# Output projection with w_out held whole in two parts, token tiles finished one by one, and a ring of 23 weight slots

## The chip, the cores and the metric

The kernel runs on one core of one Trainium2 chip. The metric is the device time of one execution in microseconds (us). The kernel before takes 1562.64 us, the median of 3 runs (1561.81 to 1563.06).

## What is computed

One encoder block on 512 tokens of width 1024, in float32: two kinds of attention, a merge, an output projection, and a mixture of 16 experts in which every expert picks its 64 tokens.

```python
h = _rms_norm(x, attn_norm_w)
z = einsum('btd,dc->btc', h, w_in)      # latent q, kv, diff q, k, v, two gates
o_mla  = 16 heads of latent attention
o_diff = 8 heads, softmax(q1 k1) - lam * softmax(q2 k2), times v
merged = sigmoid(g_mla + b0) * o_mla + sigmoid(g_diff + b1) * o_diff
x  = x + einsum('btc,cd->btd', merged, w_out)          # the output projection
h2 = _rms_norm(x, ffn_norm_w)
affinity  = softmax(einsum('btd,de->bte', h2, router_w))
gate, idx = top_k(swapaxes(affinity, 1, 2), 64)        # tokens of each expert
ye = (silu(xe @ w_gate) * (xe @ w_up)) @ w_down * gate # 16 experts, xe = h2[idx]
x  = x + scatter_add(idx, ye)
```

## The kernel before

The 512 tokens are four tiles of 128 (t = 0 to 3); the width of 1024 is eight blocks of 128 (k or c = 0 to 7). A float32 product of the first part is made of three: each operand is split into a high part of type float32r (an ACT copy) and the rest (a subtraction on DVE or POOL), and `proj3` (lines 195 to 202) sums high by high, high by low and low by high on TensorE (PE). A split of a weight is `w_split` (lines 122 to 131): load, ACT copy at line 129, subtraction at line 130.

The order of the program is: input projection and latent attention (to about 320 us), then eight differential heads (`diff_proj` projects a head's q, k and v, `diff_head` does its attention, `finish` adds it, gated, to the merge `mrg`), then the output projection and the router, then the experts. A scheduler interleaves neighbouring pieces on each engine, so that products of the output projection fill PE while head 7, the last, waits for other engines. Each engine and each DMA queue works through its list in order. Nearly all loads go through the queue of SP.

The output projection (lines 644 to 803) goes by halves of the columns, n = 0 and 1. For a half, four pieces of w_out (128x2x512, 512 KB each) are loaded and split (`wo_split`), the merge is split for each token tile into `mt` (lines 705 to 710), and 24 products per tile are summed over the eight blocks. The first half goes over k = 0 to 6 for all four tiles and then k = 7, the block of head 7. In the second half each tile is evacuated into `xm` (which holds x and becomes x plus the projection), transposed (`xm_part`) and routed (`route`: logits `lg`, softmax, `aff`, and its transpose). After the last tile a chain of maxima (`largest`, lines 805 to 816) finds the threshold of each expert, and the first expert's tokens are gathered by products with a one-hot matrix (`xeTp`, line 904).

The expert weights are 384 chunks of 1 MiB: for each expert eight of w_gate, eight of w_up, eight of w_down. `chunks()` (lines 678 to 696) issues them on SP, each into the next slot of a ring. ORDER (line 32) is a string with a letter per slot: m is the memory of the merge, h of its splits, e, a, x and b, c other places that come free at the end of the heads or of the projection. A chunk's load waits until the last reader of its slot is done; when PE has used a chunk (eight products `gu` at line 943 or `y` at line 976) its slot takes a new one. The first five chunks stand in SP's list ahead of two pieces of w_out (`raw1`, lines 700 to 702), which go through a slot of kind a.

Of the kernel before, what the change touches and what calls it, by code (L numbers as in the profile page):

```python
# [16 lines left out]
OP = mybir.AluOpType  # L17
# [14 lines left out]
ORDER = "eeeemmaxaaaahhhhbbbbbc"  # L32
NRE, NRA, NRB = (ORDER.count(c) for c in "eab")
# [13 lines left out]
def build(tc, A, out):  # L47
# [41 lines left out]
    with ExitStack() as es:  # L89
# [9 lines left out]
        wpool = prj.enter_context(tc.tile_pool(name="w", bufs=1, reuse_waits="tile"))  # L99
# [526 lines left out]
        V.tensor_tensor(rw, rw, vT[:, FN:FN + 8, None].to_broadcast([128, KT, NE]), OP.mult)  # L626

# [13 lines left out]
        pb.__exit__(None, None, None)  # L641
        pb3.close()

# [4 lines left out]
        wpool = att.enter_context(tc.tile_pool(name="wo", bufs=1, reuse_waits="tile"))  # L648

        def wo_view(n, i):  # L650
            return w_out[:, 2 * i:2 * i + 2, n * 512:(n + 1) * 512]

        def wo_split(n):
            return [w_split(wo_view(n, i), (128, 2, 512), eng=G if n == 0 and i == 3 else None,
                            raw=raw1[:, i - 2] if n == 1 and i > 1 else None) for i in range(4)]

        sc = wpool.tile([NE, 1024], F32, name="sc")
        wo0 = wo_split(0)
        mt_ = [ringH.tile([128, 2, KT, 128], F32R, name="mt", tag="wh", bufs=NT) for _ in range(NT)]
# [14 lines left out]

        def slot_tile(pool, tag, n, shape=(128, FF)):
            return pool().tile(list(shape), F32, name="w" + tag, tag=tag, bufs=n)

        def chunks():

            i = 0  # L680
            for e in range(NE):
# [3 lines left out]
                for src in srcs:  # L685
                    pool, tag, n = rings[order[i]]
                    i += 1
                    w = slot_tile(pool, tag, n)
# [8 lines left out]

        stream = chunks()
# [6 lines left out]
        for c0, c1 in ((0, 2), (2, 4), (4, 6), (6, 7), (7, 8)):  # L705
            for t in range(NT):
                hi, lo = mt_[t][:, 0, c0:c1], mt_[t][:, 1, c0:c1]
                m = mrgs[c0 // 4][:, c0 % 4:(c1 - 1) % 4 + 1, t * 128:(t + 1) * 128]
                S.activation(hi, m, AF.Copy)
                V.tensor_sub(lo, m, hi.bitcast(F32))  # L710
# [68 lines left out]
        for n in range(2):  # L779
            wo = wo0 if n == 0 else wo_split(1)  # L780
            if n == 0:
                wps = [ps_tile(g_, "wo") for g_ in ("pj", "pj", "s", "s")]
                for ks in (range(7), range(7, 8)):
                    for t in range(NT):
                        wo_part(wps[t], t, wo, ks)
                for t in range(NT):
                    wo_evac(wps[t], t, 0)
# [225 lines left out]
```

## Time and profile before

| | |
|---|---|
| median of the runs | 1562.64 us |
| lowest and highest of 3 | 1561.81 and 1563.06 us |
| the profiled execution | 1563.41 us, of which the span of the trace is 1561.7 us |
| busy in the span | PE 1436.0 us (92%), DVE 567.5 (36%), ACT 376.8 (24%), POOL 158.3 (10%) |
| moved by DMA | 448.55 MB |

The profiled execution lies 0.8 us above the median; 1.7 us of it lie outside the span. All positions below are microseconds from the span's start. PE is TensorE, DVE VectorE, ACT ScalarE, POOL GpSimd, and SPq the queue of loads that SP issues. The page cuts the span into 40 slices of 39 us; a digit there is a busy share in tenths.

### The profile page before, as it was taken

The page shows a single profiled execution, that of the slowest core. Times are in us where ns is not written, and L with a number is a line of the kernel's source. Part 1 is how long each engine was busy: PE and PEld are TensorE (multiplying, and loading weights), DVE is VectorE, ACT ScalarE, POOL GpSimd, SP SyncE. Part 2 cuts the span into 40 slices and gives each one's busy share as a digit, 9 for nine tenths or more (in the row PEclk, how much of TensorE's full clock was granted, in tenths as well). Part 3 has the DMA queues.
Part 4 walks back from the last instruction along what each step waited for, and adds up shares of the span by engine and source line. Part 5 has one row for each costly group of instructions (what it writes and reads, how often), then busy time and mean ns, then how long its engine had stood idle before and what let it go on. Part 6 is the DMA issues. An engine that isn't in the chain of part 4 may idle for free. (4 is left out here: it accounts for less than half of the span.)

```text
span 1561.7 us, 18429 instructions
## 1 busy us (share of the span) xinstructions
PE 1436.0 (92%) x7119; PEld 780.2 (50%) x7119; DVE 567.5 (36%) x1412; ACT 376.8 (24%) x830; POOL 158.3 (10%) x213
## 2 busy tenths in 40 slices
PE   8999999999999897899999979889879979979876
PEld 6776767788888676434333333223224224215211
DVE  7966646538888886202102002002002002002100
ACT  4545545536566653000000000000000000000000
POOL 3003203023434410000000000000000000000000
PEclk9999999999999999899999999999999999999999
DMA  4412113122212268899999999999999999999997
GB/s 157 128 52 62 58 35 109 38 89 61 75 49 58 69 229 319 333 421 424 420 421 424 420 421 425 422 423 421 420 423 424 419 424 423 422 423 420 419 418 293
DMA packets 125691, 448.55 MB, mean 287 GB/s; under 512 B 9734, under 2 KB 51778, under 8 KB 92579
## 3 DMA queue, kind: packets, MB, share of 16 engines
q1 hardware_dynamic: 124160, 444.30, 71.6%
q0 software_dynamic: 1440, 3.07, 0.7%
q8 instruction: 56, 0.92, 0.2%
q14 instruction: 33, 0.26, 0.0%
q10 hardware_dynamic: 2, 0.00, 0.0%
HBM read 441.57 MB, written 5.77 MB: 286 GB/s over the span
## 5 line engine op out<-in xcount | busy, mean ns | idle before, releaser
L955 DVE TENSOR_TENSOR hh<-hh,gu 128x512 f32<-128x512 f32 x32 | 22.0, 687 | 432.3 <-PE gu L943 432.3
L943 PE MATMUL gu<-wwa,xeT 128*64 128x512 f32 x560 | 129.8, 599 | 14.2 <-DMA wwa<-in_expert_w_up_dram 8.2
L943 PE MATMUL gu<-wwb,xeT 128*64 128x512 f32 x520 | 121.6, 599 | 15.6 <-DMA wwb<-in_expert_w_up_dram 8.1
L943 PE MATMUL gu<-wwe,xeT 128*64 128x512 f32 x496 | 117.5, 601 | 15.6 <-DMA wwe<-in_expert_w_up_dram 9.0
L943 PE MATMUL gu<-wwh,xeT 128*64 128x512 f32 x432 | 101.3, 599 | 11.3 <-DMA wwh<-in_expert_w_gate_dram 6.5
L952 ACT ACTIVATE hh<-gu 128x512 f32<-128x512 f32 x32 | 19.0, 597 | 343.3 <-PE gu L943 343.3
L943 PEld LDWEIGHTS gu<-wwa,xeT 128*64 128x64 f32 x560 | 37.4, 136 | 102.3 <-issue 66.2
L201 PE MATMUL dqkv<-hl,hTh 128*128 128x384 f32 x256 | 88.2, 345 | 0.3 <-DVE hl L510 0.3
L200 PE MATMUL dqkv<-hl,hTh 128*128 128x384 f32 x256 | 87.3, 342 | 0.0
L882 POOL DMA_DIRECT2D out_dram<-acc x4 | 2.2, 558 | 828.8 <-DVE acc L878 828.8
L202 PE MATMUL dqkv<-hl,hTl 128*128 128x384 f32 x256 | 85.6, 339 | 0.0
L943 PEld LDWEIGHTS gu<-wwb,xeT 128*64 128x64 f32 x520 | 34.6, 136 | 100.5 <-issue 59.6
L976 PE MATMUL y<-wwb,hh 128*64 128x512 f32 x320 | 74.1, 599 | 7.2 <-DMA wwb<-in_expert_w_down_dram 7.2
L943 PEld LDWEIGHTS gu<-wwe,xeT 128*64 128x64 f32 x496 | 32.5, 137 | 94.4 <-issue 52.8
L963 ACT ACTIVATE hh<-hTp 128x512 f32<-128x512 f32 x16 | 9.6, 597 | 277.7 <-PE hTp L960 277.7
L943 PEld LDWEIGHTS gu<-wwh,xeT 128*64 128x64 f32 x432 | 28.7, 136 | 80.8 <-issue 51.4
L976 PE MATMUL y<-wwa,hh 128*64 128x512 f32 x280 | 63.7, 597 | 4.2 <-DMA wwa<-in_expert_w_down_dram 4.0
L904 PE MATMUL xeTp<-ohr,xm 128*128 128x128 f32 x512 | 62.6, 282 | 1.3 <-DVE ohr L891 1.3
L904 PEld LDWEIGHTS xeTp<-ohr,xm 128*128 128x128 f32 x512 | 59.8, 196 | 7.6 <-issue 6.3
L875 PE MATMUL comb<-yo 128*128 128x512 f32 x112 | 57.4, 625 | 4.1 <-ACT yo L988 4.1
L989 DVE COPY yo<-y 64x512 f32<-64x512 f32 x14 | 9.7, 694 | 140.4 <-ACT yo L988 140.3
L976 PE MATMUL y<-wwh,hh 128*64 128x512 f32 x240 | 55.1, 598 | 3.6 <-DMA wwh<-in_expert_w_down_dram 3.6
(356 smaller groups left out, 2562.5 us busy)
## 6 DMA issues: line engine op xcount, KB each, us to landing
wwb<-in_expert_w_down_dram SPq DMA_DIRECT2D x39, 1024.0 KB, 18.0
wwa<-in_expert_w_gate_dram SPq DMA_DIRECT2D x36, 1024.0 KB, 19.8
wwb<-in_expert_w_up_dram SPq DMA_DIRECT2D x35, 1024.0 KB, 19.5
wwa<-in_expert_w_down_dram SPq DMA_DIRECT2D x35, 1024.0 KB, 20.0
wwa<-in_expert_w_up_dram SPq DMA_DIRECT2D x34, 1024.0 KB, 19.8
wwe<-in_expert_w_gate_dram SPq DMA_DIRECT2D x32, 1024.0 KB, 19.6
wwb<-in_expert_w_gate_dram SPq DMA_DIRECT2D x30, 1024.0 KB, 19.6
wwe<-in_expert_w_up_dram SPq DMA_DIRECT2D x30, 1024.0 KB, 19.6
```

The source lines that it names most:

```text
L200: PE.matmul(p, sh, mh, start=first and k == 0, stop=False)
L201: PE.matmul(p, sh, ml, start=False, stop=False)
L202: PE.matmul(p, sl, mh, start=False, stop=last and k == n - 1)
L875: PE.matmul(p, ohT[:, t * 128:(t + 1) * 128], ysp[:, n], start=True, stop=True)
L882: G.dma_start(out2[t * 128:(t + 1) * 128], acc[t // 2][:, t % 2])
L904: PE.matmul(p[:, k], xm[:, t, kk * 128:(kk + 1) * 128], ohr[:, t].rearrange("p a s -> p (a s)"), start=t == 0, stop=t == NT - 1)
L943: PE.matmul(pp[j][hf * 64:(hf + 1) * 64], cur[:, k, par_ * 64:(par_ + 1) * 64], wt[:, hf * 1024 + j * 512:hf * 1024 + (j + 1) * 512], star ...
L952: S.activation(hid[:, j * 512:(j + 1) * 512], pp[j], AF.Silu)
L955: V.tensor_tensor(hs, hs, gu[1][j], OP.mult)
L963: S.activation(dst, p, AF.Copy)
L976: PE.matmul(y[a * 64:(a + 1) * 64], hT[:, f, hf * 64:(hf + 1) * 64], wt[:, j, a * 512:(a + 1) * 512], start=kt == 0, stop=kt == 15)
L989: V.tensor_copy(ysp[own, 1], y[64:])
```

## The change

- The whole of w_out is held as hi and lo, in four pairs of blocks (`wo_`), instead of half of it at a time. Pair 0 is loaded and split between the latent attention and the differential heads, into a new place `ringW`. Pairs 1 and 2 are loaded raw during the heads, into the place that x will have, and split in the last heads; pair 3 is loaded late into places of the heads' tiles. The subtractions go by the rule `G if k or i == 0 else V`: five on POOL, three on DVE.
- x (`xm`) is loaded after those splits, during the last heads, instead of before the heads.
- The pool "w" of weight pieces is closed behind the latent attention and opened again as "w2".
- The merge is split in whole blocks of 512 tokens (`mt_split`), blocks 1, 3 and 5 on POOL.
- For tiles 0 and 1 the products of k = 0 to 5 are summed ahead, evacuated by ACT with the factor 0.5 and added into xm by POOL; for tile 2 they stay in PSUM. Then the tiles are finished one by one: both halves of the columns, evacuation, transposes, routing. Tile 3 has all its 48 products there. The last rsqrt of the routing is on DVE instead of POOL.
- ORDER has 23 slots in a new order; w stands for ringW. Ten chunks are issued ahead of the rest of the program's order, and no piece of w_out stands between them.
- The memory set aside for dynamic DMA is 4096 bytes instead of the default.

```diff
-ORDER = "eeeemmaxaaaahhhhbbbbbc"
-NRE, NRA, NRB = (ORDER.count(c) for c in "eab")
+ORDER = "mxeeaaaaambbbbbbhhhhwwc"
+NR = {c: ORDER.count(c) for c in ORDER}
...
+        prjw.close()
+        wpool = prjw.enter_context(tc.tile_pool(name="w2", bufs=1, reuse_waits="tile"))
...
-        xm = xpool.tile([128, NT, D], F32, name="xm")
-        for t in range(NT):
-            SY.dma_start(xm[:, t], x_in[t * 128:(t + 1) * 128])
...
+        def wo_pair(i, pool, tag, raw):
+
+            hi, lo = (pool.tile([128, 2, D], F32R, name="wo", tag=tag, bufs=NR[tag[1]]) for _ in range(2))
+            for k in range(2):
+                S.activation(hi[:, k], raw[k], AF.Copy)
+                (G if k or i == 0 else V).tensor_tensor(lo[:, k], raw[k], hi[:, k].bitcast(F32), OP.subtract)
+            return hi, lo
+
+        raw = xpool.tile([128, 2, D], F32, name="raw", tag="xm", bufs=1)
+        SY.dma_start(raw, w_out[:, 0:2])
+        wo_ = [wo_pair(0, ringW, "ww", [raw[:, k] for k in range(2)])]
+        raw = xpool.tile([128, NT, D], F32, name="raw", tag="xm", bufs=1)
+        SY.dma_start(raw, w_out[:, 2:6])
...
+        wo_ += [wo_pair(i, ringB, "wb", [raw[:, 2 * i - 2 + k] for k in range(2)]) for i in range(1, 3)]
+        xm = xpool.tile([128, NT, D], F32, name="xm", tag="xm", bufs=1)
+        for t in range(NT):
+            SY.dma_start(xm[:, t], x_in[t * 128:(t + 1) * 128])
...
+        def mt_split(c):
+            hi, lo = mth[c // 4][:, c % 4], mtl[c // 4][:, c % 4]
+            S.activation(hi, mrg(c), AF.Copy)
+            (G if c % 2 and c < 6 else V).tensor_tensor(lo, mrg(c), hi.bitcast(F32), OP.subtract)
...
+        for t in range(2):
+            for n in range(2):
+                p = ps_tile("pj", "wo")
+                wo_part(p, t, n, range(6))
+                part = mo2.tile([128, 512], F32, name="part", tag="ohr" if n else "oh", bufs=1)
+                S.activation(part, p, AF.Copy, scale=0.5)
+                xs = xm[:, t, n * 512:(n + 1) * 512]
+                G.tensor_tensor(xs, xs, part, OP.add)
+        wp2 = [ps_tile("pj", "wo") for n in range(2)]
+        for n in range(2):
+            wo_part(wp2[n], 2, n, range(6), last=False)
+        raw = [pb1p.tile([128, D], F32, name="raw", tag="qk2", bufs=2),
+               pbp.tile([128, D], F32, name="raw", tag="qkv", bufs=3)]
+        for k in range(2):
+            SY.dma_start(raw[k], w_out[:, 6 + k])
+        wo_.append(wo_pair(3, ringB, "wb", raw))
...
-        early = [next(stream) for _ in range(5)]
-        raw1 = slot_tile(*rings["a"], shape=(128, 2, 2, 512))
-        for i in range(2):
-            SY.dma_start(raw1[:, i], wo_view(1, 2 + i))
-        early += [next(stream) for _ in range(2)]
+        early = [next(stream) for _ in range(10)]
...
-            rr = rsqrt1(mo, st[:, 1:2], "rr", G if t == NT - 1 else V)
+            rr = rsqrt1(mo, st[:, 1:2], "rr")
...
+        for t in range(NT):
+            wps = wp2 if t == 2 else [ps_tile("s", "wo") for n in range(2)]
+            xT = xTs[:, t % 2]
+            for n in range(2):
+                wo_part(wps[n], t, n, range(8) if t == 3 else range(6, 8), first=t != 2)
+                if n:
+                    xm_part(t, 0, 4, xT, S)
+                wo_evac(wps[n], t, n, 1 + n)
+            xm_part(t, 4, 2, xT, V)
+            xm_part(t, 6, 2, xT, S)
+            route(t, xT)
...
-    nc = bacc.Bacc("TRN2", target_bir_lowering=False, num_devices=1)
+    nc = bacc.Bacc("TRN2", target_bir_lowering=False, num_devices=1, dynamic_dma_scratch_size=4096)
```

The list of SP, from the last pieces of w_out to the end of the first lap of slots (wm, wwx, wwe and so on are chunks in slots of those kinds, gB a gate that a head reads), before:

```order
L127 DMA wr<-in_w_out_dram 128x2x512 x4
L695 DMA wm_6081<-in_expert_w_gate_dram 128x2048
L695 DMA wwx<-in_expert_w_gate_dram 128x2048
L695 DMA wwe<-in_expert_w_gate_dram 128x2048 x4
L702 DMA wwa<-in_w_out_dram 128x2x512 x2
L695 DMA wm_6086<-in_expert_w_gate_dram 128x2048
L695 DMA wwa<-in_expert_w_gate_dram 128x2048
L695 DMA wwa<-in_expert_w_up_dram 128x2048 x4
L695 DMA wwh<-in_expert_w_up_dram 128x2048 x4
L695 DMA wwb<-in_expert_w_down_dram 128x2x1024 x5
L695 DMA wwc<-in_expert_w_down_dram 128x2x1024
L695 DMA wwe<-in_expert_w_down_dram 128x2x1024 x2
```

And now:

```order
L667 DMA xm<-in_x_dram 128x1024 x4
L698 DMA raw<-in_w_out_dram 128x1024
L740 DMA wm_6242<-in_expert_w_gate_dram 128x2048
L740 DMA wwx<-in_expert_w_gate_dram 128x2048
L740 DMA wwe<-in_expert_w_gate_dram 128x2048 x2
L740 DMA wwa<-in_expert_w_gate_dram 128x2048 x4
L740 DMA wwa<-in_expert_w_up_dram 128x2048
L740 DMA wm_6260<-in_expert_w_up_dram 128x2048
L740 DMA www<-in_expert_w_down_dram 128x2x1024
L740 DMA wwb<-in_expert_w_up_dram 128x2048 x6
L740 DMA wwh<-in_expert_w_down_dram 128x2x1024 x4
L740 DMA wwc<-in_expert_w_down_dram 128x2x1024
```

The chunks in slots of kinds h and b have changed places, x and one block of w_out stand ahead of the first chunk, and the chunk of slot w stands ahead of those of b.

The list of POOL from the last copy KH of head 6 to the last biases of head 7 (L529 and L533 normalise head 7's q and k, L564 and L568 are the biases by distance), before:

```order
L553 COPY KH<-KH 64x512
L564 TENSOR_SCALAR bias<-dist 128x512 x4
L534 TENSOR_SCALAR gB<-gB 128x512
L529 TENSOR_TENSOR qk_5730<-qkv,rq_y 128x256 x4
L130 TENSOR_TENSOR hl<-wr,hl 128x1024
L564 TENSOR_SCALAR bias<-dist 128x512 x2
```

And now (L634 is the subtraction of a w_out block, L674 that of a merge block, L691 the addition of a partial sum):

```order
L568 TENSOR_SCALAR bias<-dist 128x512 x3
L634 TENSOR_TENSOR wo<-raw,wo 128x1024
L674 TENSOR_TENSOR mt<-mrg,mt 128x512 x2
L568 TENSOR_SCALAR bias<-dist 128x512
L538 TENSOR_SCALAR gB<-gB 128x512
L634 TENSOR_TENSOR wo<-raw,wo 128x1024
L533 TENSOR_TENSOR qk_5742<-qkv,rq_y 128x256 x4
L674 TENSOR_TENSOR mt<-mrg,mt 128x512
L557 COPY KH<-KH 64x512
L691 TENSOR_TENSOR xm<-xm,part 128x512
L568 TENSOR_SCALAR bias<-dist 128x512
L634 TENSOR_TENSOR wo<-raw,wo 128x1024
L568 TENSOR_SCALAR bias<-dist 128x512
L691 TENSOR_TENSOR xm<-xm,part 128x512 x3
```

Instead of one subtraction of w_out, three of them, three of the merge and one addition now stand among the head's own steps, and three additions behind them.

The list of SP where the differential heads begin (gBd stores a gate, dist loads the distances, wr the heads' weights), before:

```order
L484 DMA gBd<-gs 128x512
L504 DMA wr<-in_w_in_dram 128x3x128 x6
L621 DMA xm<-in_x_dram 128x1024 x2
L504 DMA wr<-in_w_in_dram 128x3x128 x2
L625 DMA rw<-in_router_w_dram 128x8x16
L504 DMA wr<-in_w_in_dram 128x3x128 x4
L533 DMA gB<-gBd 128x512
L618 DMA dist<-distd 128x2048
```

And now:

```order
L626 DMA rw<-in_router_w_dram 128x8x16
L639 DMA raw<-in_w_out_dram 128x2x1024
L485 DMA gBd<-gs 128x512 x2
L508 DMA wr<-in_w_in_dram 128x3x128 x8
L508 DMA wr<-in_w_in_dram 128x3x128 x2
L537 DMA gB<-gBd 128x512
L622 DMA dist<-distd 128x2048
L508 DMA wr<-in_w_in_dram 128x3x128 x4
L642 DMA raw<-in_w_out_dram 128x4x1024
```

The first pair of w_out and two gate stores now stand ahead of the heads' first weights, and four blocks of w_out behind those of the second head.

## Rows read from the trace of the kernel before

**Rows 1.** The page: PE's line of busy time, and the slices' data rates.
```profile
PE 1436.0 (92%) x7119; PEld 780.2 (50%) x7119; DVE 567.5 (36%) x1412; ACT 376.8 (24%) x830; POOL 158.3 (10%) x213
...
DMA  4412113122212268899999999999999999999997
GB/s 157 128 52 62 58 35 109 38 89 61 75 49 58 69 229 319 333 421 424 420 421 424 420 421 425 422 423 421 420 423 424 419 424 423 422 423 420 419 418 293
```

**Rows 2.** Who waited for whom, PE, 1340 to 1440 us (total, times, longest).
```profile
PE gu L943 <- DMA wwe<-in_expert_w_gate_dram: 2.2, 4, 0.6
```

**Rows 3.** Windows: length, busy time of PE, PEld, DVE, ACT, POOL, clock, DMA share, GB/s.
```profile
540.00:560.00 20.00, 15.48 (x72) 11.56 (x73) 18.30 (x45) 10.64 (x22) 8.82 (x8) 0.91 0.43 136
560.00:610.00 50.00, 49.83 (x283) 40.98 (x282) 36.53 (x118) 21.45 (x64) 1.33 (x1) 1.00 0.83 323
610.00:670.00 60.00, 47.16 (x242) 24.55 (x242) 23.39 (x104) 5.10 (x14) 2.00 (x7) 0.86 0.85 320
```

**Rows 4.** Timeline of SP's queue, expert chunks: start, time from first to last, count.
```profile
556.69 0.34 SPq L695 DMA_DIRECT2D wm<-in_expert_w_gate_dram  x1
...
592.85 21.37 SPq L695 DMA_DIRECT2D wwh<-in_expert_w_up_dram  x4
617.04 3.38 SPq L695 DMA_DIRECT2D wwb<-in_expert_w_down_dram  x5
...
636.73 3.32 SPq L695 DMA_DIRECT2D wwe<-in_expert_w_down_dram  x2
```

**Rows 5.** Timeline of PE: the last products of the projection, and the first gate products.
```profile
613.25 0.39 PE L201 MATMUL wo<-hl,mt 128*128 128x512 f32 x1
613.47 0.39 PE L202 MATMUL wo<-hl,mt 128*128 128x512 f32 x1
...
634.61 2.08 PE L943 MATMUL gu<-wwe,xeT 128*64 128x512 f32 x8
```

**Rows 6.** Who waited for whom, PE, 520 to 614 us.
```profile
PE S L569 <- DVE QS L558: 3.1, 3, 2.6
PE pvd L591 <- DVE AT L588: 2.1, 2, 1.5
PE ATp L583 <- DVE rq_a L67: 1.2, 1, 1.2
```

**Rows 7.** Groups by line and shape, DVE, 526 to 582 us (busy us, mean ns).
```profile
L130 DVE TENSOR_TENSOR hl<-wr,hl 128x1024 fp32r<-128x1024 f32 x5 | 6.6, 1328 | 0.0
...
L710 DVE TENSOR_TENSOR mt<-mrg,mt 128x256 fp32r<-128x256 f32 x12 | 5.6, 484 | 0.0
...
L601 DVE TENSOR_SCALAR vo<-oss 128x4 f32<-128x4 f32 x2 | 2.3, 1172 | 0.8 <-ACT junk L594 0.8
...
L710 DVE TENSOR_TENSOR mt<-mrg,mt 128x128 fp32r<-128x128 f32 x6 | 1.5, 282 | 0.3 <-ACT mt L709 0.3
```

**Rows 8.** Timeline of DVE in head 7 (start, length, what it waited for).
```profile
549.62 2.17 DVE L601 TENSOR_SCALAR vo<-oss 128x4 f32<-128x4 f32 x1 [0.30 <-ACT junk L594]
...
566.87 0.68 DVE L572 CUSTOM_DVE_ANT_0 ns<-S,bias 128x512 f32<-128x512 f32 x1
```

**Rows 9.** Timeline of POOL, entry into the heads and head 7.
```profile
320.94 0.98 POOL L612 MEMSET KL<- 64x512 f32 x2 [4.68 <-PE pv L477]
...
549.38 2.39 POOL L130 TENSOR_TENSOR hl<-wr,hl 128x1024 fp32r<-128x1024 f32 x1 [2.96 <-ACT hl L129]
...
558.38 2.96 POOL L564 TENSOR_SCALAR bias<-dist 128x512 f32<-128x512 f32 x2 [5.79 <-DVE ro_a L66]
```

**Rows 10.** Timeline of SP's queue where the differential heads begin.
```profile
235.74 12.42 SPq L504 DMA_DIRECT2D wr<-in_w_in_dram  x6
...
291.20 0.44 SPq L484 DMA_DIRECT2D gBd<-gs  x1
...
321.13 0.42 SPq L533 DMA_DIRECT2D gB<-gBd  x1
332.37 8.57 SPq L504 DMA_DIRECT2D wr<-in_w_in_dram  x8
```

**Rows 11.** Timeline of PE: the first product of a differential head.
```profile
304.37 0.33 PE L200 MATMUL dqkv<-hl,hTh 128*128 128x384 f32 x1
```

More of the change, by code (lines that the diff above doesn't have):

```diff
@@ new lines, in build, with wo_part @@
+        for t in range(NT):
+            SY.dma_start(xm[:, t], x_in[t * 128:(t + 1) * 128])
+        mth, mtl = ([ringH.tile([128, KT // 2, T], F32R, name="mt", tag="wh", bufs=NR["h"]) for _ in range(2)]
+                    for _ in range(2))
+        def mt_split(c):
+            hi, lo = mth[c // 4][:, c % 4], mtl[c // 4][:, c % 4]
+            S.activation(hi, mrg(c), AF.Copy)
+            (G if c % 2 and c < 6 else V).tensor_tensor(lo, mrg(c), hi.bitcast(F32), OP.subtract)
+        def wo_part(p, t, n, ks, first=True, last=True):
+            q, d = slice(t * 128, (t + 1) * 128), slice(n * 512, (n + 1) * 512)
+            proj3(p, [(mth[k // 4][:, k % 4, q], mtl[k // 4][:, k % 4, q]) for k in ks],
+                  [(wo_[k // 2][0][:, k % 2, d], wo_[k // 2][1][:, k % 2, d]) for k in ks], first, last)
@@ new lines, in build @@
+        for c in range(6):
+            mt_split(c)
+        for t in range(2):
[7 more added lines that the diff above has]
+        wp2 = [ps_tile("pj", "wo") for n in range(2)]
@@ L641, in build @@
+        for n in range(2):
[5 more added lines that the diff above has]
+        wo_.append(wo_pair(3, ringB, "wb", raw))
+        for c in (6, 7):
+            mt_split(c)
         pb.__exit__(None, None, None)
         pb3.close()
-        prj.close()
-        ringH = es.enter_context(tc.tile_pool(name="ringH", bufs=1, reuse_waits="tile"))
@@ L648, in build @@
[L648 to L659, printed above, removed]
+        ringC = es.enter_context(tc.tile_pool(name="ringC", bufs=1, reuse_waits="tile"))
@@ L660, in build @@
+        sc1 = mo2.tile([NE, 512], F32, name="sc", tag="oh", bufs=1)
+        sc2 = mo2.tile([NE, 320], F32, name="sc", tag="ohr", bufs=1)
         ringX = es.enter_context(tc.tile_pool(name="ringX", bufs=1, side="right", reuse_waits="tile"))
@@ L685, in chunks @@
                 for src in srcs:
-                    pool, tag, n = rings[order[i]]
+                    pool, tag = rings[order[i]]
+                    w = pool.tile([128, FF], F32, name="w" + tag, tag=tag, bufs=NR[order[i]])
                     i += 1
-                    w = slot_tile(pool, tag, n)
                     if len(src.shape) == 3:
@@ L696, in chunks @@
                     yield w
+        xTs = ringC.tile([128, 2, KT, 128], F32, name="xT", tag="wc", bufs=NR["c"])
         stream = chunks()
-        early = [next(stream) for _ in range(5)]
-        raw1 = slot_tile(*rings["a"], shape=(128, 2, 2, 512))
-        for i in range(2):
-            SY.dma_start(raw1[:, i], wo_view(1, 2 + i))
-        early += [next(stream) for _ in range(2)]
-        stream = chain(early, stream)
[L705 to L710, printed above, removed]
+        early = [next(stream) for _ in range(10)]
+        stream = chain(early, stream)
         lt = cst.tile([128, 128], BF16, name="lt")
@@ L984, in build @@
             if e == 0:
-                yo = ringC.tile([128, FF], F32, name="yo", tag="wc", bufs=1)
+                yo = ringC.tile([128, FF], F32, name="yo", tag="wc", bufs=NR["c"])
                 ysp, ohT = yo[:, :1024].rearrange("p (n d) -> p n d", n=2), yo[:, 1024:1536]
```

51 lines of the change are left out of this document (14 added, 37 removed).

## Prediction

> **What bounds the kernel now.** I read the page's slices first, then PE's waits late in the run, then the stretches around the output projection. The slices show two kernels in one: until slice 14 the DMA engines are mostly idle, and from slice 18 to the end they move 419 to 425 GB/s at a busy share of 9 in every slice [rows 1]. That second part streams the expert weights: 16 experts of 24 chunks of 1 MiB, 384 chunks or 402.7 MB. At 424 GB/s a chunk takes 1.0486 / 0.424 = 2.47 us, all of them 950 us. Late in the run PE waits about half a microsecond for almost each chunk [rows 2]. So the end is: when the stream gets going, plus bytes by rate, plus a tail that the change leaves alone. PE's share of 92% deceives: it is the sum over a first part that PE bounds and a second that PE only follows.
>
> What the change can alter is therefore the start of the stream. The windows show it being lossy: 323 GB/s from 560 to 610 us, 320 from 610 to 670, and only from the next slice of the page on 420 and more [rows 1, 3]. SP's timeline says why. The first expert chunk is issued at 556.69; 1 MiB of w_out (raw1) is put in among the next; the four wwh chunks trickle out over 21 us, because their slots hold the split merge, which the last projections still read; the wwb chunks come at 617; and then nothing until 636.73, when PE has consumed its first chunk [rows 4]. In bytes: 0.323 x 50 + 0.320 x 60 = 35.35 MB, less 1.05 MB of w_out, plus the 0.62 MB that the stretch before 560 holds beyond the four w_out pieces (0.136 x 20 - 2.10): 34.9 MB of experts have landed by 670.
>
> **The sum, part by part.** Let X be the end of the last output-projection product, 613.47 + 0.39 = 613.9 [rows 5]; X' is the same point after the change.
>
> (1) Start of the stream, at an unchanged X. In the new slot order only ten chunks (m, x, two e, five a, m) have a slot that depends on nothing but the end of the heads. The other 13 lie in space that the projection still reads. The last tile alone has 48 products, in pair order; a product takes 0.22 us by the step between two neighbours [rows 5]. The whole hi/lo of pair 0 (slot w) is last read 18 products before X', so 4.1 us; the others come free from X' - 2.7 to X'. From then on SP can issue back to back; I take data as flowing from X' - 3. Those 13 chunks need 13 x 2.47 = 32 us, to X' + 29. PE frees its first slot one chunk after the first gate product: 634.61 + 2.08 = X + 22.8 [rows 5], six microseconds before that. So no second gap, and the 16 us hole in SP's list goes. By 670, with X' = X, 10.49 + 0.424 x (670 - 610.9) = 35.5 MB have landed instead of 34.9: 0.6 MB more, **-1.5 us**. That is little because the ten early chunks are through by about 585 (556.7 + 10 x 2.47 = 581, some slots a little later) and the queue is then empty for some 25 us: one hole is traded for another. Bounds: data flowing from X' - 4 or X' - 1.5, so -2.5 to 0.
>
> (2) X' itself. The projection's 192 products are the same, and PE is busy 49.83 of 50 us from 560 to 610 [rows 3]; only idle time of PE can be won. It has it before 560: 15.48 of 20 busy [rows 3], and the waits from 520 to 614 name DVE for it: 3.1 us for QS, 2.1 for AT, 1.2 for the rsqrt chain of the projections [rows 6]. The change relieves DVE there. From 526 to 582 its splits of w_out and of the merge cost 6.6 + 5.6 + 1.5 = 13.7 us [rows 7]; after it, three w_out halves (6.6 / 5 = 1.3 each) and four merge splits, 512 wide (two 256-wide ones at 0.48, so about 1, less where alone), 6.4 to 8 us. So DVE has 6 to 7 us less. If half of the 6.4 us of named waits goes: -3. Against it: the first three tiles are now finished one by one behind head 7's last transpose, each with evacuation, transposes, copies and logits on DVE and ACT, between few products; PE may wait 1 to 3 us for them; I take +1.5. Sum **-1.5**, bounds -5 and +6.5 (the second by the first rival).
>
> (3) POOL takes over: three w_out halves at 2.39 [rows 9], three merge splits and four additions of partial sums, each half as large, so about 1.2: 15.6 us, less the one 2.39 that it had, +13. Its own time is covered (8.8 of 20 busy from 540 to 560 [rows 3]). What is queued behind: the biases of head 7's last two tiles. At 558.38 they ran together [rows 9]; now an addition stands before them and a w_out half between them, so the last bias ends at 558.4 + 1.2 + 1.5 + 2.4 + 1.5 = 565. Its first user is the minimum of tile 3, at 566.87 [rows 8]: 2 us of slack, **0**, and if it were gone those 2 us would stand in the head.
>
> (4) Entry into the heads. The new pool w2 makes the first weights of the differential heads wait for gates: they are issued around 291 instead of 235.74 [rows 10], by the gate store that now stands ahead of them. The first product with them ran at 304.37 [rows 11], 13 us behind that; a load and a split fit in. The 2 MB of raw w_out then stands in SP's queue until POOL has split pair 0 behind its memsets, to 320.94 + 0.98 + 2 x 2.39 = 326.7 [rows 9]; SP's queue issued nothing between 321.13 and 332.37 [rows 10]. So **0**, bounds 0 and +4 (head 0's bias 2.6 later, a late first weight).
>
> (5) x is loaded in head 7 instead of at 261, w_out earlier: 6 MB in stretches at 136 GB/s or less; hidden. The shorter top-k behind the last tile brings the first gate product 1 us nearer to X', but by (1) six microseconds are to spare there: 0.
>
> Together -1.5 - 1.5 = -3.0 on the profiled execution's 1563.4, so 1560.4; that execution lies 0.8 above the median of 1562.64, and so **1559.6** is forecast. A difference of 0.2% (3.1 us) is about what a measurement of this kernel can tell from no change; the forecast lies on that edge.
>
> **The rivals.**
> (a) *POOL's new work blocks DVE in head 7; slower.* One row shows the price: L601, four elements wide, took 2171 ns at 549.62 [rows 8], while POOL's subtraction ran from 549.38 to 551.77 [rows 9]; the two L601 of the window average 1172 [rows 7], so the other took 0.17. It stood still for almost the whole of POOL's instruction, and PE's longest wait for QS is as long, 2.6 us [rows 6]. Had each of the three halves this effect (2.0) and each of the seven smaller operations half of it (1.0), DVE would lose 13 us where it gains 6.5: X' + 6.5, less (1): +5, 1567; with (4) at its bound 1571. It decides from the point at which more than half of POOL's added 13 us stops DVE. For it: DVE is busy 18.3 of 20 us, so hardly any of that time finds DVE idle [rows 3]. Against: POOL was busy for 8.8 of the same 20 us already [rows 3], and the means of the large groups show no such stretch: the five w_out halves took 1.33 each [rows 7].
> [...]
> (b) *The heads end much earlier*: all 6.4 us of DVE waits go and the tile-by-tile routing costs nothing: X' - 6.4, with (1) -8: 1554.6. For it: the relief equals the waits. Against: DVE is full, and a wait that goes shows the next, ACT's or PE's own chain.
> (c) *The change does not do what it says*: the stream starts as late as before, since data flows only from X' - 1.5 (the bound 0 of (1)), and the tile-by-tile routing eats the relief: 1561 to 1564. For it: one hole replaces another, and PE is full from 560 on [rows 3]. Against: the 16 us without an issue behind the wwb chunks go in any case [rows 4].
>
> **How the numbers follow.** Forecast with its spread (1557 to 1561) 0.42, (a) 0.22, (b) 0.18, (c) 0.18. Half of the forecast's case lies below 1559.5: faster 0.21 + 0.18 = 0.39; same 0.21 + 0.18 = 0.39; slower 0.22. The range reaches into the rivals on both sides until a tenth is left out at either end: 1553 (below (b)'s time, with (1) at its bound) to 1569 (the middle of (a)).
>
> **What would show it.** Right: in SP's list ten chunks by about 586, none until some 4 us before the last product, then 13 with gaps of 2.5 us and no gap before PE frees slots; 424 GB/s without a break from X' - 3; X' between 609 and 614; PE's wait for QS in head 7 gone. (a) would show as DVE instructions of 2 us and more beside POOL's in 530 to 570 and X' beyond 617; (b) as X' near 607. Wrong altogether would be a stream below 420 GB/s later on, or a PE that starves between 640 and 850 because the 23 slots are freed in another order.

## The result and the profile after

The changed kernel takes 1571.47 us, the median of 6 runs (1570.75 to 1572.0); beside it the kernel before took 1563.49 (6 runs). The ratio is 1.0051, with a 95% interval from 1.0041 to 1.0061: slower by 8 us, where 3 us less were forecast. The span of the profiled execution is 1570.24 us, 8.57 more than before.

The page, PE's line and the slices, to be read beside [rows 1]:

```profile
PE 1439.3 (92%) x7119; PEld 781.5 (50%) x7119; DVE 572.3 (36%) x1400; ACT 377.3 (24%) x822; POOL 175.2 (11%) x217
...
DMA  4412111152221064999999999999999999999997
GB/s 156 135 44 61 57 41 36 36 183 61 75 54 52 28 237 189 414 418 422 420 422 424 422 423 420 420 424 423 422 424 421 420 423 424 421 425 419 421 418 291
```

From slice 18 to the last but one both kernels move 418 to 425 GB/s. POOL has 16.9 us more. The loss lies ahead of that, and three points in PE's timeline divide it: the end of the heads' last projection product, the end X' of the last output-projection product, and the end of the last `y` product. Before they stand at 526.38, 613.86 and 1553.90 us, after at 528.07, 621.40 and 1562.48. So the heads' last projection ends 1.7 us late (1.5 of it stand already at head 0's last transposes, 389.45 beside 387.93), the stretch from there to X' is 5.85 longer (93.33 against 87.48), and from X' on it is 1.0 longer (941.08 against 940.04). That last 1.0 is no more than the scatter of one kernel: two later executions of the changed kernel have 940.08 and 941.38 there. PE's timelines, before and then after:

```profile
526.04 0.34 PE L202 MATMUL dqkv<-hl,hTl 128*128 128x384 f32 x1
...
1550.24 3.65 PE L976 MATMUL y<-wwb,hh 128*64 128x512 f32 x16 [0.55 <-DMA wwb<-in_expert_w_down_dram]
```

```profile
527.73 0.34 PE L203 MATMUL dqkv<-hl,hTl 128*128 128x384 f32 x1
...
621.01 0.39 PE L203 MATMUL wo<-wo,mt 128*128 128x512 f32 x1
...
1558.82 3.65 PE L995 MATMUL y<-wwh,hh 128*64 128x512 f32 x16 [0.51 <-DMA wwh<-in_expert_w_down_dram]
```

The last stretch first. SP's queue (start, time from first to last, count):

```profile
552.38 0.33 SPq L740 DMA_DIRECT2D wm<-in_expert_w_gate_dram  x1
...
587.48 0.33 SPq L740 DMA_DIRECT2D wm<-in_expert_w_up_dram  x1
617.10 0.38 SPq L740 DMA_DIRECT2D www<-in_expert_w_down_dram  x1
618.48 3.77 SPq L740 DMA_DIRECT2D wwb<-in_expert_w_up_dram  x6
622.30 8.61 SPq L740 DMA_DIRECT2D wwh<-in_expert_w_down_dram  x4
...
634.62 4.56 SPq L740 DMA_DIRECT2D wwc<-in_expert_w_down_dram  x1
645.67 0.37 SPq L740 DMA_DIRECT2D wm<-in_expert_w_down_dram  x1
651.58 3.30 SPq L740 DMA_DIRECT2D wwe<-in_expert_w_gate_dram  x2
```

Ten chunks by 587.5, nothing until 4.3 us before X', then thirteen, as the prediction had it. But there is a second gap: one chunk at 645.67, the next at 651.58. The windows (columns as in [rows 3]) show a dip to 376 GB/s from 660 to 670 us (403 and 363 in the two later executions):

```profile
540.00:560.00 20.00, 15.13 (x69) 12.14 (x69) 18.09 (x36) 11.96 (x24) 12.77 (x11) 0.68 0.48 185
560.00:610.00 50.00, 46.79 (x264) 37.95 (x262) 32.05 (x99) 20.30 (x61) 9.81 (x7) 1.00 0.49 190
610.00:620.00 10.00, 9.89 (x46) 7.79 (x46) 9.16 (x39) 1.72 (x6) 0.00 (x0) 1.00 0.18 49
620.00:660.00 40.00, 27.07 (x146) 16.23 (x144) 18.46 (x84) 3.62 (x9) 0.00 (x0) 0.79 1.01 414
660.00:670.00 10.00, 10.00 (x50) 3.90 (x50) 2.27 (x4) 1.20 (x2) 0.00 (x0) 1.00 0.98 376
670.00:680.00 10.00, 10.00 (x48) 3.34 (x44) 1.76 (x3) 0.00 (x0) 0.00 (x0) 1.00 1.01 420
```

The first two rows stand beside those of [rows 3]. PE, busy 49.83 of 50 us from 560 to 610 before, is now busy 46.79, and its granted clock from 540 to 560 fell from 0.91 to 0.68. What PE waited for from 520 to 625 us (total, times, longest):

```profile
PE ATp L587 <- DVE pr L584: 4.0, 2, 3.0
PE pvd L595 <- DVE AT L592: 3.2, 1, 3.2
PE ATp L587 <- DVE st L580: 2.6, 2, 1.7
PE S L573 <- DVE st L576: 1.4, 2, 1.0
...
PE S L573 <- DVE QS L562: 0.5, 2, 0.2
```

Against [rows 6] the wait for QS has gone, 3.1 to 0.5, and waits for other results of DVE have come or grown. POOL's timeline there, and DVE's beside it:

```profile
534.98 2.38 POOL L634 TENSOR_TENSOR wo<-raw,wo 128x1024 fp32r<-128x1024 f32 x1
537.32 3.46 POOL L674 TENSOR_TENSOR mt<-mrg,mt 128x512 fp32r<-128x512 f32 x2
...
544.67 2.41 POOL L634 TENSOR_TENSOR wo<-raw,wo 128x1024 fp32r<-128x1024 f32 x1
...
563.00 2.40 POOL L634 TENSOR_TENSOR wo<-raw,wo 128x1024 fp32r<-128x1024 f32 x1
```

```profile
535.95 1.42 DVE L582 SCALAR_TENSOR_TENSOR cc<-st,nlam 128x1 f32<-128x1 f32 x1
...
537.90 0.34 DVE L596 TENSOR_SCALAR o<-pvd,st 128x128 f32<-128x128 f32 x1
538.17 1.49 DVE L584 SCALAR_TENSOR_TENSOR pr<-pr,cc 128x512 f32<-128x512 f32 x1
539.58 1.24 DVE L67 TENSOR_TENSOR rq_a<-rq_a,rq_y 128x16 f32<-128x16 f32 x1
...
544.85 3.31 DVE L634 TENSOR_TENSOR wo<-raw,wo 128x1024 fp32r<-128x1024 f32 x1
...
563.69 1.73 DVE L582 SCALAR_TENSOR_TENSOR cc<-st,nlam 128x1 f32<-128x1 f32 x1
```

One column of `cc` took 1.42 and 1.73 us, and each ends where POOL's subtraction ends (537.37 beside 537.36, 565.42 beside 565.40). DVE's own half of w_out, 1.33 us long by [rows 7], went on for 1.1 us after POOL's was done at 547.08: by this reading it had stood still for nearly all of POOL's. L596, whose big operand `pvd` is in PSUM, passed in 0.34 us, and its mean in a_zero below is as long, 345 ns. This is the blocking that rival (a) names; in an experiment below (a_pool1) not every POOL instruction does it.

### The profile page after: what moved, and what is told of

It is laid out like the page before. It is cut to its first block, busy times and chain, and to the rows that moved or that the text cites. A ratio compares the mean times of both kernels' runs of the same rounds, so it can differ in the third digit from the quotient of the medians.

```text
span 1570.2 us, 18403 instructions
## 1 busy us (share of the span) xinstructions
PE 1439.3 (92%) x7119; PEld 781.5 (50%) x7119; DVE 572.3 (36%) x1400; ACT 377.3 (24%) x822; POOL 175.2 (11%) x217
## 3 DMA queue, kind: packets, MB, share of 16 engines
q0 software_dynamic: 1440, 3.07, 0.7%
## 4 chain that ended last, share of the span: by engine, by line
PE 57%; DMA 25%; DVE 10%; issue 5%; ACT 3%; POOL 0%; SPq 0%; POOLq 0%; DVEq 0%; ACTq 0%
PE gu L962 17%; PE y L995 8%; DMA wwb<-in_expert_w_gate_dram 4%; PE xeTp L923 3%; DMA wwb<-in_expert_w_down_dram 3%; PE comb L894 3%; DMA wwa<-in_expert_w_up_dram 3%; DMA wwh<-in_expert_w_up_dram 3%; DMA www<-in_expert_w_gate_dram 2%; PE pv L478 2%; DMA wwe<-in_expert_w_down_dram 2%; PE dqkv L202 2%; PE dqkv L203 2%; PE dqkv L201 2%; PE PTp L445 2%
## 5 line engine op out<-in xcount | busy, mean ns | idle before, releaser
L962 PE MATMUL gu<-wwb,xeT 128*64 128x512 f32 x656 | 153.1, 603 | 15.0 <-DMA wwb<-in_expert_w_up_dram 9.0
L962 PE MATMUL gu<-wwh,xeT 128*64 128x512 f32 x408 | 95.9, 600 | 12.0 <-DMA wwh<-in_expert_w_gate_dram 7.6
L962 PEld LDWEIGHTS gu<-wwb,xeT 128*64 128x64 f32 x656 | 44.2, 137 | 119.8 <-issue 79.7
L995 PE MATMUL y<-wwb,hh 128*64 128x512 f32 x304 | 70.0, 599 | 7.1 <-DMA wwb<-in_expert_w_down_dram 7.1
L995 PE MATMUL y<-wwa,hh 128*64 128x512 f32 x256 | 58.9, 597 | 2.3 <-DMA wwa<-in_expert_w_down_dram 2.1
L962 PE MATMUL gu<-wwe,xeT 128*64 128x512 f32 x224 | 53.4, 598 | 5.0 <-DMA wwe<-in_expert_w_up_dram 3.9
L897 DVE TENSOR_TENSOR acc<-acc,comb 128x512 f32<-128x512 f32 x48 | 33.0, 687 | 59.7 <-PE comb L894 59.7
```

The costliest lines, as they stand in the source:

```text
L897: V.tensor_tensor(a[:, sl], (a if pr else xm[:, t])[:, sl], p, OP.add)
L962: PE.matmul(pp[j][hf * 64:(hf + 1) * 64], cur[:, k, par_ * 64:(par_ + 1) * 64], wt[:, hf * 1024 + j * 512:hf * 1024 + (j + 1) * 512], star ...
L995: PE.matmul(y[a * 64:(a + 1) * 64], hT[:, f, hf * 64:(hf + 1) * 64], wt[:, j, a * 512:(a + 1) * 512], start=kt == 0, stop=kt == 15)
```

## The experiments

The points are read from PE's timelines: the end of the heads' last projection product ("entry"), X', how many of the 192 output products start before head 7's last transpose ("ahead"), and the time from X' to the end of the last `y`. Each experiment ran beside the kernel before, whose median there was 1562.89 to 1563.25; each ratio is to that. The points come from one profiled execution of each kernel, which can lie off its median: by 3.0 us above for a_x, 2.3 above for b_dve, 1.6 below for a_dve and 1.3 below for a_zero.

| kernel | median us | ratio to before, 95% | entry | X' | ahead | X' to last y |
|---|---|---|---|---|---|---|
| before | 1563.49 | | 526.38 | 613.86 | 83 | 940.04 |
| after | 1571.47 | 1.0041 to 1.0061 | 528.07 | 621.40 | 74 | 941.08 |
| a_zero | 1565.82 | 1.0005 to 1.0025 | 528.36 | 615.46 | 85 | 939.58 |
| a_dve | 1568.40 | 1.0024 to 1.0048 | 527.51 | 617.08 | 77 | 940.49 |
| b_pool | 1570.67 | 1.0032 to 1.0065 | 525.80 | 619.69 | 83 | 942.04 |
| a_pool1 | 1568.06 | 1.0015 to 1.0039 | 526.99 | 616.97 | 74 | 941.69 |
| b_dve | 1562.37 | 0.9991 to 1.0010 | 525.90 | 614.46 | 68 | 940.83 |
| a_pad | 1573.31 | 1.0042 to 1.0076 | 529.09 | 622.44 | 74 | 941.28 |
| a_now2 | 1573.62 | 1.0051 to 1.0082 | 529.50 | 622.99 | 74 | 941.41 |
| a_dve_now2 | 1568.96 | 1.0024 to 1.0054 | 528.94 | 619.24 | 77 | 940.81 |
| a_dve_add_now2 | 1570.16 | 1.0026 to 1.0057 | 529.04 | 620.57 | 69 | 940.51 |
| a_raw4 | 1572.07 | 1.0035 to 1.0068 | 527.21 | 621.42 | 74 | 940.04 |
| a_x | 1571.38 | 1.0027 to 1.0061 | 531.21 | 624.64 | 74 | 939.68 |
| a_dve_raw4_x | 1566.35 | 1.0011 to 1.0030 | 527.37 | 617.67 | 77 | 939.25 |
| a_zero_raw4_x | 1563.43 | 0.9995 to 1.0013 | 526.64 | 613.50 | 85 | 939.45 |

**POOL's late subtractions left out, or on DVE.** In the expectations "lock" stands for rival (a), DVE held by POOL's subtractions, and "covered" for (3) of the forecast.

```diff
-                (G if k or i == 0 else V).tensor_tensor(lo[:, k], raw[k], hi[:, k].bitcast(F32), OP.subtract)
+                if k and i:
+                    S.activation(lo[:, k], raw[k], AF.Copy, scale=0.0)
+                else:
+                    (G if i == 0 else V).tensor_tensor(lo[:, k], raw[k], hi[:, k].bitcast(F32), OP.subtract)
```

> The changed kernel in which the low parts that POOL subtracts in the last heads (second block of w_out pairs 1 to 3, merge blocks 1, 3 and 5) are left out: ACT writes zeros in their place, so these low parts are missing from the projection's sum. POOL's late subtractions go and DVE gets nothing. Lock: DVE's instructions of 1.2 to 3.3 us beside POOL's go, the projection ends 4 to 5 us earlier, about 1567. Covered (rival): same as the changed kernel, 1571.5. If ACT's 5 us of extra copies delay head 7, a little later than either.

That is a_zero; a_dve has instead:

```diff
+                (G if i == 0 else V).tensor_tensor(lo[:, k], raw[k], hi[:, k].bitcast(F32), OP.subtract)
```

> The changed kernel with the late subtractions (one w_out half of pairs 1 to 3, merge blocks 1, 3 and 5) on DVE instead of POOL; the partial-sum additions stay on POOL. If POOL's two-operand subtractions stop DVE (theory: lock), DVE takes about 3 x 1.2 + 3 x 0.7 = 5.7 us of work and loses some 8 us of standing still: the end of the projection 1 to 3 us earlier, 1568.5 to 1570.5. If DVE is simply full in head 7 and POOL's work was covered (rival): 3 to 6 us later, 1574.5 to 1577.5.

(Merge blocks 1, 3 and 5, at line 674, are changed in the same way in both.)

Left out, X' comes 5.9 us earlier though the entry is no better, and the median falls by 5.7. On DVE, X' comes 4.3 earlier and the median falls by 3.1. The intervals of a_dve and after overlap, but eight of the nine runs of a_dve lie below every run of after. So about half of the cost is that the work sits on POOL: head 7 is through earlier although DVE does more itself. All this is a little more than was expected of either run. The granted clock differs too. From 540 to 550 us, after and then a_zero:

```profile
540.00:550.00 10.00, 5.15 (x21) 4.08 (x21) 10.00 (x21) 6.26 (x12) 6.99 (x5) 0.50 0.06 17
```

```profile
540.00:550.00 10.00, 7.25 (x46) 5.78 (x46) 7.91 (x17) 7.54 (x16) 6.56 (x6) 1.00 0.44 143
```

It was 0.50 in after and 1.00 in a_zero. In the 10 us before, PE had been busy 5.76 us in after and 7.11 in a_zero; but a_pool1, with 7.01 there, was granted 0.58 from 540 to 550, and a_x, with 8.48, was granted 0.65. So what sets the clock is not shown, and what of the 5.7 us goes by way of it was not separated.

**Useless subtractions on POOL in the kernel before.**

```diff
+                if 4 * h + t >= 26:
+                    for _ in range(2):
+                        jp = pbnp.tile([128, T], F32, name="jp", tag="jp", bufs=1)
+                        G.tensor_tensor(jp, AT, dist[:, t], OP.subtract)
```

> The kernel before with twelve useless POOL subtractions of 512 columns (AT minus a distance tile, into a spare tile), two per token tile from the third tile of head 6 to the end of head 7: about 15 us of POOL work, as much as the change adds, and nothing else changed. Lock: DVE stands still for part of it, 3 to 6 us later, 1566.5 to 1569.5. Covered (rival): 1563.5. What head-of-line waiting of POOL's own biases adds shows as waits of DVE for bias.

These are twelve subtractions whose results nobody uses, 16.8 us of POOL's time, and the median rose by 7.6 us where 3 to 6 were expected; in the profiled execution head 7's last transpose came 6.1 later, X' 5.8, and the stretch behind X' was 2.0 longer, which is not explained. In its trace, POOL and DVE:

```profile
546.90 4.30 POOL L592 TENSOR_TENSOR jp<-AT,dist 128x512 f32<-128x512 f32 x3
```

```profile
550.10 1.38 DVE L714 TENSOR_TENSOR mt<-mrg,mt 128x256 fp32r<-128x256 f32 x1
```

A merge split of 0.48 us [rows 7] took 1.38. So POOL's two-operand work in head 7 costs such an amount without the new order too; what of it went through the steps of POOL queued behind it was not separated.

**The same POOL time with one operand.**

```diff
+                if k and i:
+                    G.tensor_scalar(lo[:, k], raw[k], 0.0, None, op0=OP.mult)
...
+            if c % 2 and c < 6:
+                G.tensor_scalar(lo, mrg(c), 0.0, None, op0=OP.mult)
```

> The changed kernel with POOL's six late subtractions replaced by multiplications by zero of the one raw operand (the low parts that they make are left out of the sum). POOL stays as busy or busier in head 7, but reads one SBUF operand instead of two. If only a POOL instruction with two SBUF operands stops DVE: DVE's instructions of 1.2 to 3.3 us go and the time is that of the run with zeros from ACT, 1566 to 1567. If any POOL instruction stops DVE, or POOL's queue delays head 7's biases: 1571 or more.

POOL is busy as long as in after (its instructions add up to 34.4 us against 33.4, from 520 us to 3 us behind head 7's last transpose). DVE's groups from 526 to 586 us (busy us, mean ns) in after:

```profile
L584 DVE SCALAR_TENSOR_TENSOR pr<-pr,cc 128x512 f32<-128x512 f32 x8 | 7.1, 882 | 0.0
L634 DVE TENSOR_TENSOR wo<-raw,wo 128x1024 fp32r<-128x1024 f32 x3 | 6.6, 2196 | 0.0
L582 DVE SCALAR_TENSOR_TENSOR cc<-st,nlam 128x1 f32<-128x1 f32 x8 | 4.4, 552 | 0.0
L674 DVE TENSOR_TENSOR mt<-mrg,mt 128x512 fp32r<-128x512 f32 x4 | 3.5, 887 | 0.0
...
L67 DVE TENSOR_TENSOR rq_a<-rq_a,rq_y 128x16 f32<-128x16 f32 x3 | 2.0, 657 | 0.0
```

In a_zero:

```profile
L584 DVE SCALAR_TENSOR_TENSOR pr<-pr,cc 128x512 f32<-128x512 f32 x8 | 5.9, 743 | 0.0
L637 DVE TENSOR_TENSOR wo<-raw,wo 128x1024 fp32r<-128x1024 f32 x3 | 4.1, 1354 | 0.6 <-ACT wo L633 0.6
...
L582 DVE SCALAR_TENSOR_TENSOR cc<-st,nlam 128x1 f32<-128x1 f32 x8 | 1.7, 210 | 0.0
...
L67 DVE TENSOR_TENSOR rq_a<-rq_a,rq_y 128x16 f32<-128x16 f32 x3 | 0.9, 297 | 0.0
```

In a_pool1, and behind them one pair of its timelines, POOL and DVE:

```profile
L637 DVE TENSOR_TENSOR wo<-raw,wo 128x1024 fp32r<-128x1024 f32 x3 | 4.8, 1609 | 0.0
...
L582 DVE SCALAR_TENSOR_TENSOR cc<-st,nlam 128x1 f32<-128x1 f32 x8 | 2.0, 253 | 0.0
```

```profile
540.54 2.82 POOL L635 TENSOR_SCALAR wo<-raw 128x1024 fp32r<-128x1024 f32 x1
```

```profile
540.72 1.98 DVE L637 TENSOR_TENSOR wo<-raw,wo 128x1024 fp32r<-128x1024 f32 x1
...
555.81 0.96 DVE L66 SCALAR_TENSOR_TENSOR ro_a<-vo,ro_y 128x4 f32<-128x4 f32 x1
```

DVE's subtraction ran and ended inside POOL's instruction, 0.6 us longer than its 1.35, where beside a two-operand one it took 3.31 us and ended 1.1 after POOL's. So it is not POOL's time alone that holds DVE to the end of an instruction, but what POOL runs; the number of operands and the operation (TENSOR_TENSOR, TENSOR_SCALAR) changed together here. The median is 3.4 us below after. A one-operand instruction is not free for DVE either: four elements a partition (L66) took 0.96 us beside the multiplication from 555.73 to 558.49, against a mean of 159 ns in after. That a_pool1 remains 2.2 us above a_zero, between the two times expected, is not explained: such shorter holds, POOL's other steps that wait behind its work, and the clock, 0.58 from 540 to 550, may each have a part.

**The one subtraction that POOL had before, on DVE.**

```diff
-            return [w_split(wo_view(n, i), (128, 2, 512), eng=G if n == 0 and i == 3 else None,
+            return [w_split(wo_view(n, i), (128, 2, 512), eng=None,
```

> The kernel before with its one late subtraction on POOL (the last w_out piece, 2.39 us at 549.38) on DVE instead. Lock: the 2.17 us that a four-element operation took beside it goes, DVE does 1.2 us more, PE's wait of 2.6 us for QS shrinks: 0.5 to 1.5 us earlier than the kernel before, 1562 to 1563, which would beat both. Rival (that wait was DVE's load, not POOL): 1 us later.

Head 7's last transpose comes 2.7 us earlier (576.48 against 579.15), but only 68 products are then ahead of it instead of 83, and X' is 0.6 later. What the head gains, the filler loses; the median is that of before within its interval.

**The entry into the heads.** In after the first weights of the heads are issued at 305.69, not 291, and the 2 MB of raw w_out go at 327.06, ahead of later weights. SP's queue:

```profile
305.69 9.66 SPq L508 DMA_DIRECT2D wr<-in_w_in_dram  x8
...
327.06 0.37 SPq L642 DMA_DIRECT2D raw<-in_w_out_dram  x1
...
333.81 6.67 SPq L508 DMA_DIRECT2D wr<-in_w_in_dram  x6
```

Two runs tried the pool of weights. The first puts a spare tile into w2, so that its pieces lie clear of the last gate's splits:

```diff
+                hl = wpool.tile([128, 2, 2, 384], F32R, name="hl", tag="hl", bufs=5)
+                if h == 0 and i == 0:
+                    pad = wpool.tile([128, 3200], F32, name="pad", tag="pad", bufs=1)
...
-                hl = wpool.tile([128, 2, 2, 384], F32R, name="hl", tag="hl", bufs=5)
```

> The changed kernel with the weight pieces of pool w2 placed so that they do not lie over the splits that the last gate product reads: the first weights of the differential heads need not wait for that product any more (305.7 us), only for the gate store ahead of them in SP's list (about 291). Theory entry (late first weights cost 1.7 us at head 0 and this is handed on to the end): 1.2 to 1.7 us earlier, 1570. Rival (the loss at the entry is made up, or is POOL's splitting of pair 0 in front of head 0's bias): 1571.5.

The second keeps the pool of the first part open:

```diff
-        prjw.close()
-        wpool = prjw.enter_context(tc.tile_pool(name="w2", bufs=1, reuse_waits="tile"))
```

> The changed kernel without the closing and reopening of the weight pool: the differential heads' first weights are loaded at 235 to 262 us again, as before, and no load waits for the last gate product. Entry theory (1.5 us are lost there and handed on): head 0's last transpose back to about 388, the whole about 1.5 us earlier, 1570. If the 2 MB load of raw w_out among head 1's weights is the loss, it stays: 1571.5.

Both missed: entry 1.0 and 1.4 us later than after. Yet the edits did what they were to do: the first weight is issued at 290.88 in a_pad and at 235.07 in a_now2, and in a_now2 the heads' first product runs at 303.76, against 309.76 in after and 304.37 before. So late first weights alone do not explain the late entry. In a_now2 PE waited 2.3 us for a weight that stood behind the raw load. So the raw load was cut into four, behind the projections of heads 1 to 4 (the copy of one column only sets when a load may start):

```diff
-        SY.dma_start(raw, w_out[:, 2:6])
...
+            if 1 <= h < 5:
+                V.tensor_copy(raw[:, h - 1, 0:1], res[h][0][:, 0, 0:1])
+                SY.dma_start(raw[:, h - 1], w_out[:, h + 1])
```

> The changed kernel with the 2 MB load of raw w_out (blocks 2 to 5), which stands in SP's list at 327 us ahead of the weights of heads 1 and 2, cut into four loads of 512 KB, one behind each of the projections of heads 1 to 4 (a one-column copy on DVE ties each to its head). New theory of the entry: that load, not the pool, makes PE wait for the heads' weights (2.3 us where the pool was not reopened). Then head 0's last transpose comes at 388.0 to 388.5 instead of 389.45 and the whole is 1 to 1.5 us earlier, 1570 to 1570.5. Rival (the loss is the late first weights after all): 1571.5, or later if each of the four loads delays its own head.

The entry is 0.9 us earlier than after, X' is not (621.42), and the time is the same. As the gain was of the size of the scatter between kernels, both ran twice more:

> The changed kernel again, for where head 0's last transpose falls (389.45 in its first profile). If the 2 MB load makes the heads' weights land late by chance: anywhere from 388.4 to 392.6, as in the seven profiles so far that have that load. If it is a fixed delay: 389.3 to 389.6 again.

> The same kernel as in the run before it, a second draw, with the same two expectations: 388.4 to 392.6 by chance, or 389.3 to 389.6 fixed.

> The changed kernel with that load cut into four, again. If the one load is the cause: 388.7 to 388.8 again, with no wait of PE for a head's weights over 0.7 us. If the scatter has another cause: as wide as with the load in one.

> The same kernel as in the run before it, a second draw, with the same two expectations: 388.7 to 388.8 again, or as wide as with the load in one.

After: entry 528.11 and 527.73, X' 622.09 and 621.14 (1571.88 and 1572.47 us). Cut in four: 527.57 and 527.26, X' 620.76 and 620.96 (1571.07 and 1570.88). So cutting is worth half a microsecond on average at the entry, and as much at X', where the two ranges overlap. Head 0's last transposes begin at 389.45, 389.46 and 389.21 in after and at 388.75, 389.20 and 388.57 in a_raw4: neither kernel repeats itself as closely as was expected of a fixed cause, and the two ranges all but meet. The rest of the late entry stays, and its cause was not found.

**Without the reopened pool, with DVE subtractions; and the additions on DVE too.** The second also adds the partial sums from PSUM, without POOL:

```diff
-                part = mo2.tile([128, 512], F32, name="part", tag="ohr" if n else "oh", bufs=1)
-                S.activation(part, p, AF.Copy, scale=0.5)
...
-                G.tensor_tensor(xs, xs, part, OP.add)
+                V.scalar_tensor_tensor(xs, p, 0.5, xs, OP.mult, OP.add)
```

> Both undone: POOL's late subtractions on DVE, and the weight pool not reopened. If the two losses add up: the run with the subtractions on DVE (1568.4) less 1.1 to 1.5, about 1567; what is left over the kernel before is then the tail of the projection (2 us more behind head 7's last transpose) and the stream. If the entry's loss is swallowed by head 7's own waits: 1568.4 again.

> As the last, and the partial sums are added into x by DVE straight from PSUM (one operation of 0.69 us each) instead of by ACT's copy and POOL's addition: no POOL work at all is added in head 7. If the four additions on POOL (1.29 each) still hold DVE up or hold PSUM too long: 1 to 2 us earlier than the last, 1565 to 1566. If DVE is then the one that is late: the same or 1 us later.

The first is a_dve with a later entry: 1568.96, and not the 1567 of two gains that add up. The second is no faster (X' 1.3 us later than in the first): taking the additions off POOL gained nothing here, with only 69 products ahead.

**x as the tenth slot.**

```diff
-ORDER = "mxeeaaaaambbbbbbhhhhwwc"
+ORDER = "meeaaaaamxbbbbbbhhhhwwc"
```

> The changed kernel with the slot of kind x as the tenth of the ring instead of the second. The slot of x takes no second chunk, so the 25th chunk waits for PE's third chunk, and PE's first eight chunks come at 2.95 us each against 2.47 for a load. If the dip to 376 GB/s from 660 to 670 us is that, it goes: about 1 us earlier, 1570.5. Rival (the dip is DMA noise or the loads' landing order): the same, 1571.5.

```profile
660.00:670.00 10.00, 10.00 (x53) 4.09 (x53) 2.56 (x5) 0.00 (x0) 0.00 (x0) 1.00 1.01 425
```

The dip is gone (425 for 376), and X' to the last `y` is 1.4 us shorter than in after's first execution. One pair says little: the three kernels with x moved have 939.25 to 939.68 there, the thirteen executions of the changed kernel without it 939.58 to 941.69, so 1.2 us by the means; and a_zero, in which SP's list has the same gap of 5.9 us, is as short as those with x moved (939.58) and moves 403 GB/s or more in every 5 us from 640 to 670. The median is as in after: by itself the edit gained nothing that the runs show. The profiled execution lies 3.0 us above that median and its entry is 3.1 us late, the latest among kernels that load the raw 2 MB at once (526.99 to 531.21).

**Together.** a_dve_raw4_x joins the edits of a_dve, a_raw4 and a_x; a_zero_raw4_x those of a_zero, a_raw4 and a_x.

> All three repairs: late subtractions on DVE, raw w_out in four loads, x as the tenth slot. If the losses are separate they add: 1568.4 less 1.1 for the entry and less 1 for the stream, 1566 to 1566.5; what remains over the kernel before is PE's idle time in head 7 (2 us more than before). Rival (they hide one another): 1568.

> The kernel after with all three suspected costs taken away together: POOL's six late two-operand subtractions left out (their low parts are written as zeros by ACT, so those low parts are missing from the products), the raw load of w_out cut in four behind heads 1 to 4, and x as the tenth slot. If the three causes are all there is to the loss, the time is that of the kernel before or less: the left-out subtractions alone gave 1565.8, the other two together took 2.0 us from the version with DVE subtractions (1568.4 to 1566.4), so 1563.8, with the end of the last product at 614 or earlier and no dip of the data rate behind it. If something else in the change costs time too, the result stays at 1565 or more, or the repairs of the entry are swallowed again before the last product (its end stays at 615.5).

With all three away the time is that of the kernel before, X' too (613.50). From after, 5.7 us went with the subtractions and 2.4 with the edits for entry and x together (alone, neither of these moved the median), against the 8.0 that had been lost. But this kernel leaves out six subtractions whose like the kernel before makes. With the work kept, on DVE, 1566.35 remain, 3.2 above before: in the kernel before DVE does nearly as much splitting (13.7 us by [rows 7], 15.0 in a_dve) at no such price, with 83 products ahead instead of 77. What in the new order leaves DVE's work uncovered was not tried, so this part of the cause stays open. No version beats the kernel before.

## Why the prediction was wrong

- **(3), POOL's added work at 0, is the step that failed.** The amount was right: POOL's groups from 526 to 586 us have 7.2 + 5.2 + 5.2 us of subtractions and additions less the one of 2.4, 15 us where 13 were worked out. The queue behind was right as well: the last bias began at 565.37 (its end was forecast for 565) and was not waited for. But "its own time is covered" looked for who waits for POOL, and the price was on DVE, which POOL held. With the subtractions left out 5.7 us go (a_zero); 3.4 of them go already when POOL stays as busy with one operand (a_pool1), and 3.1 when DVE does the work itself (a_dve). Useless subtractions on POOL in the kernel before cost 7.6 (b_pool).
- **(2), −1.5, came out at +5.85**, or +7.5 for X' with the entry. The relief of 6 to 7 us was counted with subtractions at the length that they have alone. The two groups took 6.6 + 3.5 = 10.1 us, so 3.6 less than before's 13.7; and three groups lost 8 x 0.34 + 8 x 0.14 + 3 x 0.36 = 4.9 us against a_zero (L582, L584, L67). Most of it lies on the chain from `cc` over `pr` to the transposes, for which PE's waits have grown.
- **Rival (a)** named this mechanism and priced it at 1567, with a late entry at 1571; it came to 1571.47. The mechanism was right; that the sum came out so near is in part luck, as the entry gave 1.7 of its 4 us and the stream behind X' gained nothing of the 1.5 counted on. It was given too little because the large groups of before showed no stretched mean. That was the wrong row: before, one POOL subtraction could meet them. The row that counted was L601, four elements wide and 2.17 us long [rows 8], and beside it [rows 9].
- **(4), entry at 0 with bounds 0 and +4, measured +1.7.** The weights were issued at 305.69, not 291, but issuing them earlier did not help (a_pad, a_now2). The raw load ahead of the next weights is part of the cause (half a microsecond by a_raw4 and its repeats).
- **(1), −1.5, measured +1.0, and 0.0 and +1.3 in two later executions: no gain.** Ten chunks, the hole, thirteen back to back came as worked out. "No second gap" failed: x's slot takes one chunk in the whole run, so the second slot to come free helped nobody, and the first freed slot stood at X' + 24.3. With x moved, 0.4 to 0.8 us are gained against the one execution of before (939.68, 939.25, 939.45 for 940.04): about half of the forecast at most, and within the scatter.
- **(5), 0, held**: no wait for x or w_out shows among PE's, and from slice 18 on the stream is as before.

## What to carry to other kernels

Moving work to an engine that seems idle is priced by what it does to its neighbours too (5.7 of the 8.0 us lost here went with POOL's six subtractions): before giving POOL a subtraction of two SBUF operands beside a DVE that is busy 18 of 20 us, look in the trace for a tiny DVE instruction that is as long as POOL's (before: four elements in 2.17 us beside POOL's 2.39 [rows 8, 9]). When a ring of slots is reordered, follow the second lap as well as the first, and ask of every slot whether it takes a chunk again. A head that ends earlier gains nothing if the work that filled its waits is left over behind it (b_dve: the head 2.7 us earlier, X' 0.6 later).

## What was not expected of the hardware

That it matters so much what POOL runs, and not only how long: beside POOL's 128x1024 subtraction (2.4 us) DVE's own took 3.31 us and a single column 1.73, while beside a POOL multiplication of the same shape, longer at 2.8 us, DVE's took 1.98, and L582's mean was 253 ns against 210 with the work left out and 552 beside subtractions. Whether the second operand decides or the kind of operation was not separated, and the multiplication held a small DVE instruction for up to 0.8 us too (L66).
